# Token mixing in groups of 512 columns, convolution sums in PSUM, and 256-column products throughout a decoder layer

## The chip, the cores and the metric

One Trainium2 chip, of which the kernel uses one core. The metric is the device time of one execution in microseconds. Engines are named as in the profile: PE multiplies matrices, ACT (ScalarE), DVE (VectorE) and POOL (GpSimd) work element by element, SP issues transfers.

## The reference

One decoder layer on 256 tokens of width 2048, in fp32:

```python
f = swiglu_ffn(rms_norm(h, ffn1_pre_g), ffn1_w_gu, ffn1_w_down)        # d_ff 5632
h = h + 0.5 * rms_norm(f, ffn1_post_g)
z = rms_norm(h, mix_pre_g) @ w_in                                      # 2048 x 5120
a, g, q, k, v = split(z, 5 x 1024)
conv_out = silu(layer_norm(causal_depthwise_conv31(a * sigmoid(g))))   # 1024 channels
attn = moba_attention(rope(q), rope(k), v)       # 8 heads; 256 tokens are one block: causal attention
h = h + rms_norm(concat(conv_out, attn) @ w_out, mix_post_g)
h = h + rms_norm(memory_cross_attention(rms_norm(h), rms_norm(mem)), xattn_post_g)
f = swiglu_ffn(rms_norm(h, ffn2_pre_g), ffn2_w_gu, ffn2_w_down)
return h + 0.5 * rms_norm(f, ffn2_post_g)
```

## The kernel before

All weights come from HBM once, as tiles of 128 x 1024 fp32 (`raw`, 512 KB each), through one queue of SP. Each tile is split into two parts in a reduced format that PE multiplies in one pass: `hi` is written by ACT (`split_hi`, L177 without and L179 with a gain per row), `lo` = raw - `hi` by DVE (`split_lo`, L193 without, L195 with a gain). Activations are split likewise (chunks `ck`, parts 0 and 1). A product of the layer is then three on PE: hi with hi, hi with lo, lo with hi. `Weights` prepares `hi` three tiles and `lo` two tiles ahead of use.

A **step** is one weight tile: `step(mm, k)` takes it, issues its 24 products of 256 columns (or the like) and then lets a background queue (`Background`, `bg`) issue pieces for the other engines: pieces of the main queue up to the next `cut`, and then taps of the convolution as far as a credit per engine allows. Each engine executes its instructions in the order in which they are issued.

The stages are gate-up of the first feed-forward network (22 groups of 512 columns, weights stationary, `gate_up`), its down projection (tokens stationary, `proj` and `down`, two halves of 44 tiles), a boundary with residual, norm and transposes (`boundary`, with key products of the cross-attention as fillers), token mixing, cross-attention, and the second feed-forward network.

In gate-up the first two groups use `proj_T`, products of 256 columns. All others multiply a `hi` weight with both activation parts at once, 512 columns (L636), and `lo` with part 0, 256 columns (L638). The halves are added afterwards (`add_parts`, L596 and L597).

Token mixing multiplies four groups for the gated product (`glu_group`, 256 channels each), then queries and keys of four heads (1024 columns, four PSUM banks), all values (four banks), and queries and keys of the other four heads. The convolution has 31 taps on 8 tiles of 128 channels. For the even tiles a tap is one DVE operation on SBUF (`tap_dve`, L746: cv = yv * w + cv). For the odd ones ACT multiplies (L756) and POOL adds (L757), through a ring of three products. `queue_ln` normalises the result, `queue_rope` rotates queries and keys, `queue_heads` runs the attention of four heads in stages. All of these share the main queue. The output projection (`down`) takes the convolution's 8 tiles first and then the heads.

Of the kernel before, what the change touches and what calls it, by code (L numbers as in the profile page):

```python
# [14 lines left out]
P = 128  # L15
# [12 lines left out]
RAW, HI, LO, TMP = 4, 4, 3, 2  # L28
STEP_DVE, STEP_ACT, STEP_POOL = 1.2, 1.3, 2.4
TAIL = 3  # L30
X_AT = [0, 1, 3, 5]
MEM_AT = [20, 22, 24, 26]
# [10 lines left out]
class Background:  # L43


    def __init__(self):
        self.main = deque()
        self.dve = deque()
        self.pool = deque()
        self.credit = [0.0, 0.0, 0.0]  # L50

    def add(self, fn, dve=0.0, act=0.0, pool=0.0):
        self.main.append((fn, dve, act, pool))

    def cut(self):
        self.main.append(None)

    def urgent(self, pieces):

        for fn, dve, act in reversed(pieces):  # L60
            self.main.appendleft(None)
            self.main.appendleft((fn, dve, act, 0.0))
# [5 lines left out]
    def step(self):  # L68
        self.credit = [min(c + d, d) for c, d in zip(self.credit, (STEP_DVE, STEP_ACT, STEP_POOL))]
        while self.main:  # L70
            p = self.main.popleft()
            if p is None:
                break
            p[0]()
            self.spend(*p[1:])
        while self.dve and self.credit[0] > 0:
            self.dve.popleft()()
            self.spend(0.4, 0.0, 0.0)
        while self.pool and self.credit[1] > 0 and self.credit[2] > 0:
            self.pool.popleft()()  # L80
            self.spend(0.0, 0.4, 0.7)

    def flush(self):
        while self.main:
            p = self.main.popleft()
            if p is not None:
                p[0]()
# [136 lines left out]
def layer_kernel(ctx: ExitStack, tc: tile.TileContext, x, mem, eye, consts, smalls, post_g, xt, memt,  # L224
# [15 lines left out]
    def chunk(dt=F32R):  # L240
        if dt == F32R:
            return ap.tile([P, 4, 2, 256], F32R, tag="chunk", bufs=15, name="ck")
        return ap.tile([P, 2048], F32, tag="chunk", bufs=15, name="cf")
# [51 lines left out]
    for n in range(32):  # L295
        u = 2 * (n % 8)
        W.add(w_in[n // 16, n % 16], [S_GM + u, S_GM + u + 1])
    for g in (3, 2, 4):
        for k in range(KT):
            W.add(w_in[g, k], [S_GM + k])  # L300
    for hf in range(2):
        for k in range(KT):
            W.add(w_out[hf, k])
            kv_extra(1, hf, k, KV_AT2)
# [47 lines left out]
    class Rows:  # L352


        def __init__(self, src, key=None):
            self.src = src
            self.key = key
            self.xT = [None] * 4
# [11 lines left out]
        def hi(self, t, c):  # L370
            make_hi(self.part(t, c, 0), self.ps[t, c])

        def lo(self, t, c):
            make_lo(self.part(t, c, 1), self.ps.pop((t, c)), self.part(t, c, 0))
# [43 lines left out]
    def proj_T(regions, first, last, hi, lo, xk, parts_first=False):  # L418
# [10 lines left out]
    def proj(pss, first, last, hi, lo, xk, t, n0=0):  # L429

        xs = [xk[:, f, t * P:(t + 1) * P] for f in (0, 1, 0)]
        for n, ps in enumerate(pss):
            for o in (0, 256):
                c = slice((n0 + n) * 512 + o, (n0 + n) * 512 + o + 256)
# [822 lines left out]
```

## Time and profile before

| | |
|---|---|
| median of 3 runs | 1967.59 us (1964.88 to 1969.87) |
| profiled execution, its own time | 1969.58 us |
| its span, first to last instruction | 1967.8 us |
| PE, DVE, ACT, POOL busy | 97%, 65%, 56%, 10% of the span |
| mean granted clock of PE | 0.995 |
| gate-up of the first network | 57.5 to 500.2 us |
| its down projection | 500.2 to 740.0 us |
| token mixing with its output projection | 753.3 to 1130.8 us |

Products on PE are pipelined: the time of one overlaps the next, so the pace of a stretch is read from the starts of its instructions or from their number in a stretch, not from the mean time of one. An instruction that crosses the edge of a stretch counts in both.

### The profile page before, as it was taken

Reading aid. Unit: us, or ns where it says so; the run is one execution under the profiler, and the core shown is the slowest. Engines: PE = TensorE matmul, PEld = TensorE weight load, DVE = VectorE, ACT = ScalarE, POOL = GpSimd, SP = SyncE. Lnnn points to the kernel's source line nnn. Section 1 sums busy time; section 2 is a strip of 40 time slices with the busy share of each in tenths; the row PEclk is TensorE's granted clock in tenths of the full one; section 3 lists DMA queues with packets and bytes.
Section 4 is the critical chain, followed back from the end, with each engine's and each line's share of the span. In section 5 each row is a group of like instructions: output and inputs, shape, how many; then the busy total and the mean of one; then the engine's idle time right before and its main releaser. Section 6 shows DMA issues by size and latency. Waiting matters only on the chain.

```text
span 1967.8 us, 34797 instructions
## 1 busy us (share of the span) xinstructions
PE 1913.8 (97%) x13818; PEld 1794.8 (91%) x13818; DVE 1269.5 (65%) x1774; ACT 1098.5 (56%) x1793; POOL 205.0 (10%) x192
## 2 busy tenths in 40 slices
PE   8999999999999999888999999999999999999998
PEld 8888888888999999877899999988888888899998
DVE  5666666666545557999767676666666666654444
ACT  6655555555434646766465565655556555543433
POOL 0000000000000000768401000000000000000000
PEclk9999999999999999999999999999999999999999
DMA  8555566555656774444555653555655555666564
GB/s 286 191 192 187 190 192 193 189 189 191 215 194 194 265 246 139 131 149 140 168 164 163 223 179 122 171 190 189 191 191 192 189 188 191 209 198 194 194 193 149
DMA packets 102116, 369.98 MB, mean 188 GB/s; under 512 B 11456, under 2 KB 11712, under 8 KB 101184
## 3 DMA queue, kind: packets, MB, share of 16 engines
q1 hardware_dynamic: 100944, 361.00, 56.5%
q10 hardware_dynamic: 1008, 6.75, 0.9%
q8 instruction: 108, 1.77, 0.4%
q14 instruction: 56, 0.46, 0.1%
HBM read 365.61 MB, written 2.10 MB: 187 GB/s over the span
## 4 chain that ended last, share of the span: by engine, by line
PE 89%; DVE 5%; issue 2%; POOL 2%; ACT 1%; DMA 1%; SPq 0%; DVEq 0%; POOLq 0%; ACTq 0%
PE ps L436 31%; PE ps L636 30%; PE ps L638 15%; PE ps L423 7%; PE ps L426 3%; DVE lo L195 3%; DVE cv L746 2%; POOL cv L757 1%; PE ps L339 0%; DMA raw<-in_f_gu_dram 0%; ACT hi L179 0%; PE ps L1079 0%; DMA raw<-in_xt_dram 0%; PE ps L1077 0%; PE ps L1078 0%
## 5 line engine op out<-in xcount | busy, mean ns | idle before, releaser
L195 DVE SCALAR_TENSOR_TENSOR lo<-raw,sm,hi 128x512 fp32r<-128x512 f32 (+1 forms) x830 | 636.8, 806 | 336.6 <-issue 249.1
L179 ACT ACTIVATE hi<-raw,sm 128x512 fp32r<-128x512 f32 (+1 forms) x830 | 576.2, 740 | 379.4 <-PE ps L636 223.1
L636 PE MATMUL ps<-ck,hi 128*128 128x512 f32 x2560 | 693.6, 393 | 0.0
L436 PE MATMUL ps<-hi,ck 128*128 128x256 f32 x3584 | 619.0, 279 | 1.3 <-ACT ck L347 1.0
L436 PEld LDWEIGHTS ps<-hi,ck 128*128 128x128 f32 x3584 | 545.7, 189 | 2.0 <-ACT ck L347 1.2
L436 PE MATMUL ps<-lo,ck 128*128 128x256 f32 x1792 | 499.5, 279 | 8.6 <-DVE lo L195 6.8
L636 PEld LDWEIGHTS ps<-ck,hi 128*128 128x128 f32 x2560 | 434.8, 188 | 54.7
L193 DVE TENSOR_TENSOR lo<-raw,hi 128x1024 fp32r<-128x1024 f32 x216 | 265.7, 1231 | 266.4 <-PE ps L436 230.8
L638 PEld LDWEIGHTS ps<-ck,lo 128*128 128x128 f32 x2560 | 388.4, 188 | 53.7
L638 PE MATMUL ps<-ck,lo 128*128 128x256 f32 x2560 | 400.0, 278 | 0.0
L177 ACT ACTIVATE hi<-raw 128x1024 fp32r<-128x1024 f32 x216 | 229.1, 1062 | 289.1 <-PE ps L436 241.0
L436 PEld LDWEIGHTS ps<-lo,ck 128*128 128x128 f32 x1792 | 339.5, 189 | 9.8 <-DVE lo L195 7.6
L423 PE MATMUL ps<-ck,hi 128*128 128x256 f32 x1664 | 230.1, 284 | 9.5 <-ACT hi L140 5.6
L423 PEld LDWEIGHTS ps<-ck,hi 128*128 128x128 f32 x1664 | 210.9, 190 | 10.8 <-ACT hi L140 5.6
L605 POOL TENSOR_TENSOR tmp<-tmp,rb 128x512 f32<-128x512 f32 x44 | 58.5, 1329 | 1127.3 <-ACT tmp L604 1108.0
L426 PE MATMUL ps<-ck,lo 128*128 128x256 f32 x832 | 130.4, 285 | 23.4 <-DVE lo L195 23.4
L426 PEld LDWEIGHTS ps<-ck,lo 128*128 128x128 f32 x832 | 111.5, 190 | 28.3 <-DVE lo L195 28.3
L757 POOL TENSOR_TENSOR cv<-cv,cf 128x255 f32<-128x255 f32 (+14 forms) x120 | 106.3, 887 | 31.9 <-ACT cf L756 23.5
L746 DVE SCALAR_TENSOR_TENSOR cv<-yv,cf,cv 128x255 f32<-128x255 f32 (+14 forms) x120 | 85.0, 708 | 2.7
L597 DVE TENSOR_TENSOR tmp<-ps,tmp 128x256 f32<-128x256 f32 x160 | 60.1, 417 | 10.8 <-ACT tmp L596 10.8
L756 ACT ACTIVATE cf<-yv,cf 128x255 f32<-128x255 f32 (+14 forms) x120 | 54.6, 487 | 16.5 <-POOL cv L757 16.1
L347 ACT ACTIVATE ck<-tmp 128x512 fp32r<-128x512 f32 x44 | 27.8, 632 | 50.2 <-DVE tmp L608 50.2
(136 smaller groups left out, 837.7 us busy)
## 6 DMA issues: line engine op xcount, KB each, us to landing
raw<-in_f_gu_dram SPq DMA_DIRECT2D x351, 512.0 KB, 4.2
raw<-in_f_down_dram SPq DMA_DIRECT2D x176, 512.0 KB, 4.3
raw<-in_w_in_dram SPq DMA_DIRECT2D x80, 512.0 KB, 3.5
raw<-in_w_out_dram SPq DMA_DIRECT2D x32, 512.0 KB, 3.6
cf<-in_post_g_dram ACTq DMA_DIRECT2D x4, 1024.0 KB, 6.6
raw<-in_x_k_dram SPq DMA_DIRECT2D x8, 512.0 KB, 4.4
raw<-in_x_q_dram SPq DMA_DIRECT2D x8, 512.0 KB, 4.1
raw<-in_x_o_dram SPq DMA_DIRECT2D x8, 512.0 KB, 4.2
```

The costliest lines, as they stand in the source:

```text
L177: self.nc.scalar.activation(dst, src, AF.Copy)
L179: self.nc.scalar.activation(dst, src, AF.Copy, scale=g)
L193: self.nc.vector.tensor_tensor(dst, src, hi.bitcast(F32), ALU.subtract)
L195: self.nc.vector.scalar_tensor_tensor(dst, src, g, hi.bitcast(F32), ALU.mult, ALU.subtract)
L423: nc.tensor.matmul(ps[:, o:o + 256], hi[:, j * P:(j + 1) * P], xk[:, f, :], start=first and o == 0 and f == 0, stop=False, skip_group_chec ...
L426: nc.tensor.matmul(ps[:, o:o + 256], lo[:, j * P:(j + 1) * P], xk[:, 0, :], start=False, stop=last, skip_group_check=True)
L436: nc.tensor.matmul(ps[:, o:o + 256], xs[i], w[:, c], start=first and o == 0 and i == 0, stop=last and i == 2, skip_group_check=True)
L597: nc.vector.tensor_tensor(s[:, c], ps[:, 0:256], s[:, c], ALU.add)
L636: nc.tensor.matmul(ps, hi[:, w], xk, start=k == 0, stop=False, skip_group_check=True)
L638: nc.tensor.matmul(ps[:, 256:512], lo[:, w], xk[:, 0, :], start=False, stop=k == KT - 1, skip_group_check=True)
L746: nc.vector.scalar_tensor_tensor(cv[:, ct, s:], yv[:, ct, :S - s], w, cv[:, ct, s:], ALU.mult, ALU.add)
L757: nc.gpsimd.tensor_tensor(cv[:, ct, s:], cv[:, ct, s:], pr[:, :S - s], ALU.add)
```

## The change

- **Gate-up:** all groups use `proj_T`, 256 columns a product, three products per weight tile of 128 x 128 and two PSUM banks a group. `add_parts` is gone: DVE multiplies straight from PSUM.
- **Order in `proj_T`:** for each PSUM region the three products (hi, hi, lo) follow each other. Before, eight `hi` products came first and four `lo` products after them.
- **Halved products:** at given steps (`HALVED`), products number 0, 4 and 8 are split into two of 128 columns each: in gate-up in the groups 1 and 2, in each down projection at two tiles of the first half, in each mixing group at one tile. These are 54 products.
- **Mixing groups:** ten groups of 512 columns with 8 tiles each: four gated ones, then queries and keys of two heads twice, values of four heads, and the same again. The pre-norm gain of mixing goes into the activations (`Rows`, four operations of 128 columns per part in place of one of 512), so that weight tiles are split without a gain.
- **Convolution:** the even channel tiles sum up in two PSUM banks (`tap_acc`): ACT writes tap 1 with the bias, DVE adds the taps 2 to 30 in PSUM and writes the last sum with tap 0 to SBUF.
- **Background:** two lanes (`lanes`), one for the normalisation of the convolution, other rates per step (`MIX_RATE`, `TAP_DVE`), and pieces cut so that each engine's part of a chain has a step of its own. The product `yv` and the last add of the rotation move from POOL to DVE.
- **Output projection:** the heads 0 to 3 come first, then the convolution, then the heads 4 to 7 (`OUT_ORDER`).
- Four temporaries in place of two, 16 chunks in place of 15, and a smaller scratch space for transfers make room.

```diff
+MIX_RATE = (1.45, 1.6, 2.5)
+TAP_DVE = 0.47
+OUT_ORDER = [8, 9, 10, 11, 0, 1, 2, 3, 4, 5, 6, 7, 12, 13, 14, 15]
+HALVED = (0, 4, 8)
...
-    for n in range(32):
-        u = 2 * (n % 8)
-        W.add(w_in[n // 16, n % 16], [S_GM + u, S_GM + u + 1])
-    for g in (3, 2, 4):
-        for k in range(KT):
-            W.add(w_in[g, k], [S_GM + k])
+    for n in range(10):
+        for u in range(8):
+            W.add(w_in[n, u])
...
+            for k in range(4):
+                nc.scalar.activation(hi[:, k], src[:, k], AF.Copy, scale=self.gain_of(c, k))
...
-        order = [(f, r) for f in range(2) for r in enumerate(regions)]
-        if not parts_first:
-            order = [(f, r) for r in enumerate(regions) for f in range(2)]
-        for f, (j, (ps, o)) in order:
-            nc.tensor.matmul(ps[:, o:o + 256], hi[:, j * P:(j + 1) * P], xk[:, f, :],
-                             start=first and o == 0 and f == 0, stop=False, skip_group_check=True)
-        for j, (ps, o) in enumerate(regions):
-            nc.tensor.matmul(ps[:, o:o + 256], lo[:, j * P:(j + 1) * P], xk[:, 0, :],
-                             start=False, stop=last, skip_group_check=True)
+        order = [(r, i) for r in enumerate(regions) for i in range(3)]
+        if parts_first:
+            order = [(r, i) for i in range(3) for r in enumerate(regions)]
+        for n, ((j, (ps, o)), i) in enumerate(order):
+            w = 128 if n in halved else 256
+            for a in range(0, 256, w):
+                nc.tensor.matmul(ps[:, o + a:o + a + w], (hi, hi, lo)[i][:, j * P:(j + 1) * P], xk[:, i % 2, a:a + w],
+                                 start=first and o == 0 and i == 0 and a == 0, stop=last and i == 2,
+                                 skip_group_check=True)
...
+                    at = HALVED if t == 0 and (hf, n) in ((0, 1), (0, 5)) else ()
+                    proj(pss[t], n == 0, n == nk - 1, hi, lo, lhs(order[n]), t, 0, at)
...
-                    for ps, w in zip(pss, ws):
-                        nc.tensor.matmul(ps, hi[:, w], xk, start=k == 0, stop=False, skip_group_check=True)
-                    for ps, w in zip(pss, ws):
-                        nc.tensor.matmul(ps[:, 256:512], lo[:, w], xk[:, 0, :], start=False, stop=k == KT - 1,
-                                         skip_group_check=True)
+                    proj_T(regions_of(pss), k == 0, k == KT - 1, hi[:, e * 512:], lo[:, e * 512:], rows.x(k),
+                           g == k == 0, HALVED if e == 0 and (g, u) in ((1, 1), (2, 1)) else ())
...
+    def tap_acc(ct, s):
+
         w = whalf[:, ct * TAPS + TAPS - 1 - s:ct * TAPS + TAPS - s]
-        if s == 0:
-            nc.vector.tensor_scalar(cv[:, ct, :], yv[:, ct, :], w,
-                                    sm[:, S_CB + ct:S_CB + ct + 1], ALU.mult, ALU.add)
+        a = acc[ct // 4][:, (ct % 4) * 128:(ct % 4) * 128 + 256]
+        b = sm[:, S_CB + ct:S_CB + ct + 1]
+        if s == 1:
+            nc.scalar.activation(a[:, 1:], yv[:, ct, :S - 1], AF.Identity, scale=w, bias=b)
+            nc.scalar.activation(a[:, 0:1], b, AF.Copy)
         else:
-            nc.vector.scalar_tensor_tensor(cv[:, ct, s:], yv[:, ct, :S - s], w, cv[:, ct, s:],
-                                           ALU.mult, ALU.add)
+            o = a[:, s:] if s else cv[:, ct, :]
+            nc.vector.scalar_tensor_tensor(o, yv[:, ct, :S - s], w, a[:, s:], ALU.mult, ALU.add)
...
+    for c in range(2):
+        for p in range(2):
+            pss = in_group(lambda u: norm_conv(c == 1 and p == 1 and u == 5))
+            if p == 0:
+                qk.append(chunk(F32))
+            queue_rope(pss, p, qk[c])
+        v_group(c, lambda u: norm_conv(False))
+        queue_heads(range(4 * c, 4 * c + 4))
     post = Post(1, 1.0)
```

DVE in the mixing stage, in the second gated group, before: two low halves of a weight tile with a gain (`lo`), then three taps into the SBUF sums (`cv`), and so on.

```order
L195 SCALAR_TENSOR_TENSOR lo<-raw,sm,hi 128x512 x2
L746 SCALAR_TENSOR_TENSOR cv<-yv,cf,cv 128x245
L746 SCALAR_TENSOR_TENSOR cv<-yv,cf,cv 128x244
L746 SCALAR_TENSOR_TENSOR cv<-yv,cf,cv 128x243
L195 SCALAR_TENSOR_TENSOR lo<-raw,sm,hi 128x512 x2
```

The same place now, around the gate (L789) and the product (L793, L794) of the second group.

```order
L197 TENSOR_TENSOR lo<-raw,hi 128x1024
L756 SCALAR_TENSOR_TENSOR ps<-yv,cf,ps 128x241
L756 SCALAR_TENSOR_TENSOR ps<-yv,cf,ps 128x240
L756 SCALAR_TENSOR_TENSOR ps<-yv,cf,ps 128x239
L197 TENSOR_TENSOR lo<-raw,hi 128x1024
L789 TENSOR_TENSOR tmp<-ps,rb 128x512
L756 SCALAR_TENSOR_TENSOR ps<-yv,cf,ps 128x238
L756 SCALAR_TENSOR_TENSOR ps<-yv,cf,ps 128x237
L197 TENSOR_TENSOR lo<-raw,hi 128x1024
L793 SCALAR_TENSOR_TENSOR tmp<-tmp,ps 128x512
L794 TENSOR_TENSOR yv<-tmp,rb 128x512
L197 TENSOR_TENSOR lo<-raw,hi 128x1024
```

One operation of 1024 columns stands where two of 512 stood; there are still three taps a step, on `ps` now; a step with a gate or a product has fewer or none.

PE in gate-up, before, at the step from the second group (L423, L426) to the third (L636, L638).

```order
L423 MATMUL ps<-ck,hi 128x256 x8
L426 MATMUL ps<-ck,lo 128x256 x4
L636 MATMUL ps<-ck,hi 128x512 x4
L638 MATMUL ps<-ck,lo 128x256 x4
L636 MATMUL ps<-ck,hi 128x512 x4
```

PE now, in the second group, at a step with halved products (128x128).

```order
L443 MATMUL ps<-ck,lo 128x256
L443 MATMUL ps<-ck,hi 128x128 x2
L443 MATMUL ps<-ck,hi 128x256
L443 MATMUL ps<-ck,lo 128x256
L443 MATMUL ps<-ck,hi 128x256
L443 MATMUL ps<-ck,hi 128x128 x2
L443 MATMUL ps<-ck,lo 128x256
L443 MATMUL ps<-ck,hi 128x256 x2
L443 MATMUL ps<-ck,lo 128x128 x2
L443 MATMUL ps<-ck,hi 128x256 x2
L443 MATMUL ps<-ck,lo 128x256
```

Each `lo` product now follows its two `hi` products, and three of these twelve are two instructions each.

DVE at the end of mixing, now: the last centred and scaled piece of the convolution (L949), its low parts (L351), and the values of the second half (L1022) that the heads 4 to 7 need.

```order
L949 TENSOR_TENSOR cv<-cv,cf 128x512
L351 TENSOR_TENSOR ck<-cv,ck 128x2x256
L197 TENSOR_TENSOR lo<-raw,hi 128x1024
L351 TENSOR_TENSOR ck<-cv,ck 128x2x256
L197 TENSOR_TENSOR lo<-raw,hi 128x1024
L351 TENSOR_TENSOR ck<-cv,ck 128x2x256
L197 TENSOR_TENSOR lo<-raw,hi 128x1024
L1022 TENSOR_SCALAR cf<-ps,scal_9256 128x512
L1022 TENSOR_SCALAR cf<-ps,scal_9262 128x512
```

The last low part stands behind the 82nd low half of mixing, whose input projection has 80 tiles; the low halves run two tiles ahead of PE.

## Rows read from the trace of the kernel before

**Rows 1.** The page, part 1: busy time, share of the span, instructions.

```profile
PE 1913.8 (97%) x13818; PEld 1794.8 (91%) x13818; DVE 1269.5 (65%) x1774; ACT 1098.5 (56%) x1793; POOL 205.0 (10%) x192
```

**Rows 2.** Stretches: length, busy time (instructions) of each engine, clock, DMA share, GB/s.

```profile
100.00:150.00 50.00, 50.00 (x292) 43.90 (x291) 33.42 (x55) 29.02 (x52) 2.62 (x2) 1.00 0.59 192
550.00:600.00 50.00, 50.00 (x443) 50.00 (x443) 22.70 (x19) 19.44 (x19) 0.00 (x0) 1.00 0.60 195
...
800.00:850.00 50.00, 41.75 (x336) 39.92 (x336) 49.26 (x66) 32.05 (x64) 33.43 (x39) 1.00 0.45 142
850.00:900.00 50.00, 39.98 (x320) 38.12 (x320) 49.22 (x57) 35.86 (x63) 40.23 (x44) 1.00 0.43 144
900.00:950.00 50.00, 38.77 (x275) 36.95 (x276) 46.26 (x48) 29.67 (x46) 40.63 (x38) 0.90 0.38 127
950.00:1000.00 50.00, 50.00 (x410) 49.75 (x410) 39.09 (x44) 26.66 (x30) 8.87 (x4) 0.97 0.60 190
```

**Rows 3.** Waits, 790 to 925 us: total us, times, longest.

```profile
PE ps L426 <- DVE lo L195: 23.4, 24, 1.4
```

**Rows 4.** Groups by shape, DVE, 790 to 925 us: count, busy us, mean ns.

```profile
L195 DVE SCALAR_TENSOR_TENSOR lo<-raw,sm,hi 128x512 fp32r<-128x512 f32 x38 | 38.2, 1044 | 0.0
...
L783 DVE TENSOR_TENSOR tmp<-ps,rb 128x512 f32<-128x512 f32 x3 | 2.1, 684 | 0.0
L787 DVE SCALAR_TENSOR_TENSOR tmp<-tmp,ps 128x512 f32<-128x512 f32 x3 | 2.0, 679 | 0.0
```

**Rows 5.** Groups, DVE: gate-up 100 to 480, down 510 to 650, all taps.

```profile
L195 DVE SCALAR_TENSOR_TENSOR lo<-raw,sm,hi 128x512 fp32r<-128x512 f32 x276 | 195.0, 748 | 126.8 <-issue 107.0 <-ACT ck L347 14.1 <-PE ps L638 5.7
L597 DVE TENSOR_TENSOR tmp<-ps,tmp 128x256 f32<-128x256 f32 x70 | 26.3, 417 | 4.4 <-ACT tmp L596 4.4
...
L193 DVE TENSOR_TENSOR lo<-raw,hi 128x1024 fp32r<-128x1024 f32 x51 | 62.5, 1226 | 73.5 <-PE ps L436 72.1 <-issue 0.9 <-ACT tmp L344 0.6
...
L746 DVE SCALAR_TENSOR_TENSOR cv<-yv,cf,cv 128x255 f32<-128x255 f32 (+14 forms) x120 | 85.0, 708 | 2.7
```

**Rows 6.** Timeline of DVE, 939 to 952 us: start, us, instruction.

```profile
939.30 3.61 DVE L746 SCALAR_TENSOR_TENSOR cv<-yv,cf,cv 128x243 f32<-128x243 f32 x3
...
949.58 1.45 DVE L746 SCALAR_TENSOR_TENSOR cv<-yv,cf,cv 128x237 f32<-128x237 f32 x3
```

**Rows 7.** Timeline of PE: early gate-up, start and end of its 512-column part, later stretch.

```profile
33.03 1.11 PE L423 MATMUL ps<-ck,hi 128*128 128x256 f32 x8
33.97 0.63 PE L426 MATMUL ps<-ck,lo 128*128 128x256 f32 x4
34.44 1.11 PE L423 MATMUL ps<-ck,hi 128*128 128x256 f32 x8
...
57.49 1.08 PE L636 MATMUL ps<-ck,hi 128*128 128x512 f32 x4
...
500.17 0.41 PE L436 MATMUL ps<-hi,ck 128*128 128x256 f32 x2
...
1247.12 1.07 PE L423 MATMUL ps<-ck,hi 128*128 128x256 f32 x8
1248.03 0.62 PE L426 MATMUL ps<-ck,lo 128*128 128x256 f32 x4
1248.48 1.07 PE L423 MATMUL ps<-ck,hi 128*128 128x256 f32 x8
```

**Rows 8.** Stretches of 10 us: down projection, value projection.

```profile
510.00:520.00 10.00, 10.00 (x90) 10.00 (x90) 4.63 (x5) 3.88 (x4) 0.00 (x0) 1.00 0.58 181
969.00:979.00 10.00, 10.00 (x88) 10.00 (x86) 7.86 (x9) 5.66 (x7) 6.01 (x3) 1.00 0.54 175
```

**Rows 9.** Timeline of PE: transposes of 128 columns at the boundary.

```profile
742.94 1.04 PE L339 MATMUL ps<-ident,h 128*128 128x128 f32 x8
743.73 0.72 PE L423 MATMUL ps<-ck 128*128 128x256 f32 x4
```

**Rows 10.** Groups by shape, ACT, whole span: high parts from PSUM.

```profile
L347 ACT ACTIVATE ck<-ps 128x512 fp32r<-128x512 f32 x24 | 13.8, 588 | 21.6 <-PE ps L339 21.6
...
L347 ACT ACTIVATE ck<-ps 128x256 fp32r<-128x256 f32 x12 | 4.3, 375 | 4.6 <-PE ps L866 4.2 <-PE ps L1099 0.5
```

More of the change, by code (lines that the diff above doesn't have):

```diff
@@ L718, in layer_kernel @@
     last = down(KF, lambda k: hT[k // 4][:, k % 4], post, ffn1_hook)
-    rows = Rows(h_rows)
+    rows = Rows(h_rows, gain=S_GM)
     boundary(post, last, rows, kv_k(0))
+    bg.rate = MIX_RATE
     mx = chunk(F32)
@@ L787, in product, with taps @@
             nc.vector.scalar_tensor_tensor(box[0], box[0], 1.0, pss[0], ALU.add, ALU.mult)
[L788 removed]
+            nc.vector.tensor_tensor(yv[:, 2 * q:2 * q + 2, :], two(box[0]), bc2(rows.rb), ALU.mult)
+        def taps():
+            gated.append(q)
+            for s in [*range(2, TAPS), 0]:
+                bg.dve.append(lambda s=s: tap_acc(2 * q, s))
             for s in range(TAPS):
[L790 removed]
@@ L931, in act, with first, split @@
                                      bias=sm[:, S_LB + ct:S_LB + ct + 1])
-        bg.add(sums, pool=3.7)
-        bg.cut()
+        def first():
+            cT[0:2] = [chunk(), chunk()]
+        def split(i, low):
+            c = slice(2 * (i % 2), 2 * (i % 2) + 2)
+            if not low:
+                make_hi(cT[i // 2][:, c, 0, :], cv[:, 2 * i:2 * i + 2, :])
+                return
+            make_lo(cT[i // 2][:, c, 1, :], cv[:, 2 * i:2 * i + 2, :], cT[i // 2][:, c, 0, :])
+        bg.lane = 1
+        bg.add(sums, dve=0.6, pool=1.2)
         bg.cut()
@@ L971, in layer_kernel @@
+        bg.cut()
+        bg.add(first)
+        for i in range(6):
+            if i < 4:
+                bg.add(lambda i=i: act(i), dve=0.7, act=1.0)
+            if 0 < i < 5:
+                bg.add(lambda i=i: split(i - 1, False), act=0.6)
+            if i > 1:
+                bg.add(lambda i=i: split(i - 2, True), dve=0.7)
+            bg.cut()
+        bg.lane = 0
     for q in range(4):
         glu_group(q)
-    pss = in_group()
-    qk.append(chunk(F32))
-    queue_rope(pss, qk[0], False)
@@ L977, in layer_kernel, with norm_conv @@
-    vps = [[bank() for _ in range(2)] for _ in range(2)]
-    def mm_v(k, hi, lo):
-        for t in range(2):
-            proj(vps[t], k == 0, k == KT - 1, hi, lo, rows.x(k), t)
-    normed = False
-    for k in range(KT):
-        step(mm_v, k)
-        if not normed and (k == 10 or not (bg.dve or bg.pool)):
+    normed = []
+    def norm_conv(last):
+        if len(gated) == 4 and not normed and (last or not (bg.dve or bg.pool)):
             bg.flush_taps()
             queue_ln()
-            normed = True
@@ L1007, in layer_kernel, with v_group, mm, v_rows @@
-    post = Post(1, 1.0)
-    last = down(KT, lambda k: cT[k // 4][:, k % 4], post)
+            normed.append(True)
+    def v_group(c, hook):
+        vps = [bank() for _ in range(2)]
+        def mm(u, hi, lo):
+            for e in range(2):
+                k = 2 * u + e
+                for t in range(2):
+                    proj([vps[t]], k == 0, k == KT - 1, hi[:, e * 512:], lo[:, e * 512:], rows.x(k), t)
+        for u in range(8):
+            step(mm, u)
+            hook(u)
+        if c == 0:
+            vms.append(chunk(F32).rearrange("p (t c) -> p t c", t=2))
+        def v_rows(t):
+            nc.vector.tensor_scalar(vms[0][:, t, c * 512:(c + 1) * 512], vps[t], rows.rs[t], None, ALU.mult)
+        for t in range(2):
+            bg.add(lambda t=t: v_rows(t), dve=0.6)
+        bg.cut()
@@ L1011, in layer_kernel @@
+    last = down(KT, lambda k: cT[k // 4][:, k % 4], post, done_hook, order=OUT_ORDER)
+    bg.rate = (STEP_DVE, STEP_ACT, STEP_POOL)
     rows = Rows(h_rows)
```

277 lines of the change are left out of this document (134 added, 143 removed).

## The prediction

> **What bounds the kernel now.** I read the page's engine totals first: the reader is to see PE busy 97% of the span, so only PE's pace and PE's pauses can be worth much [rows 1]. Then the stretches of 50 us. A gate-up stretch and a down stretch leave PE no pause; four stretches of the mixing stage do, and DVE is busy 49.3 of 50 us in two of them [rows 2]. The waits there name the releaser: PE's products with the low half of a weight tile wait for DVE's L195, 23.4 us in 24 waits [rows 3]. So two things are to be priced: the pace of products in gate-up, and DVE's load in the mixing stage.
>
> Pace. Products of 256 columns run at two rates. Twelve take 1.41 us in the first groups of gate-up (33.03 to 34.44) and 1.36 us in a later stretch of the same line (1247.12 to 1248.48) [rows 7]: 117.5 ns and 113.3 ns each. A down stretch starts 90 in 10 us; the value projection, the same code, 88 [rows 8]. The rate stays through a stretch and changes at its edges. The granted clock is 1.00 on both sides [rows 8], the 2.4 GHz level, so it isn't the clock.
>
> Loss in mixing. A step is one weight tile, 24 products. From 800 to 1000 us, 336 + 320 + 275 + 410 = 1341 products started; at 117.5 ns they need 157.6 us, so 42.4 of 200 us are lost. In 900 to 950 the granted clock averages 0.90 after PE's pauses: part of it at 1.2 GHz, whose price is inside the 42.4 [rows 2].
>
> **The change, part by part.**
>
> Gate-up, all products 256 columns. From 57.49 to 500.17 us the first gate-up does 1280 pairs (512 + 256 columns): 345.8 ns a pair, 1.383 us for four [rows 7]. A pair becomes three products of 256: 340.0 ns at the fast rate, 352.5 at the slow one. That is -5.8 or +6.7 ns times 1280, twice (the second feed-forward network repeats it): **-14.9 or +17.2 us**. The row shows twelve fast products (3072 columns) in 1.36 us where four pairs, the same columns in eight products, take longer: a third product carries no price of its own there. The Trainium skill (TensorE: Matmul & The Clock Gate, Back-to-back issue gap) gives a warm product N/2.4 + 2.5 ns: 215.8 + 109.2 for a pair, 327.5 for three, so by it the edit costs 2.5 ns 2560 times, 6.4 us, instead of gaining. The rows are slower than that formula either way, and the sum goes by the rows. I take the fast rate: the new order (high, high, low in one PSUM region, then the next) is the down projection's, where it held. Against it: the weights stay the stationary operand, as in the slow stretch of rows 7. What the two gates drop on ACT and DVE (copies and adds of halves) lies beside PE, which never paused there.
>
> Halved products: 54 are split into two of 128 columns (12 in gate-up, 18 in the three down projections, 24 in mixing). Nearest row: eight transposes of 128 columns take 0.79 us, 0.10 us each [rows 9], so a pair costs 0.20 for 0.113: +0.09 x 54 = **+4.9 us**. The low bound is 0 (half the columns, half the time), the high one 10, twice the row's excess. They are the only disturbance put inside otherwise even stretches, so the rate after them may differ from that before.
>
> Mixing, DVE per step. Before: two low halves of 512 columns at 1.044 us and three taps at 0.708 us: 4.21 us, against 2.82 us of products [rows 4, 5]. Both prices are swollen: the low half takes 0.748 in gate-up [rows 5], and three taps take 3.61 us at 939 but 1.45 at 949, ten us later [rows 6]. But in the stretch where low halves are swollen, DVE's operations with one operand in PSUM take 684 and 679 ns for 512 columns [rows 4], less than the swollen 1.044. So what swells is the pair of SBUF operands. The new taps read the sum from PSUM and write it back; no row has DVE writing PSUM. The nearest is DVE's add of a PSUM and an SBUF operand, 256 columns: 0.417 us [rows 5]; the far bound is today's 0.708. The low half, now without a gain, is one operation of 1024 columns: 1.226 us in the down stretch [rows 5], swollen by 1.044/0.748 at most 1.71. Per step: 2.48 us at best, 1.71 + 3 x 0.417 = 2.96 likely at worst, 1.71 + 3 x 0.708 = 3.83 if PSUM doesn't help; PE needs 2.72 at the fast rate. 124 taps at three a step make 41 steps: 0, 10 or 45 us left of the 42.4. I take 6, the middle of the first two and 1 for PSUM banks (two are held by the sums; PE may wait for one while heads overlap a group). **-36.4 us**. If PE's DVE wait goes, the next that can be late is ACT, whose products for the Pool taps wait for Pool ahead of the next weight's high half in the queue.
>
> Order around it: the normalisation runs in a lane of its own, and in the changed order its last piece on DVE stands at about the first tile of the output projection, which needs the convolution only at its fifth; the heads 4 to 7, needed at the thirteenth, end just before it. So I add no wait. The gated product and the rotation's last add move from Pool to DVE (4 + 8 operations of about 0.68 us, about 8 us) and take the place of taps in their steps, over more steps.
>
> Mixing, rate: in eight groups the steps after the halved products (6 x 24 x 8 = 1152) can run 4.2 ns faster: 4.8 us; the heads' own products cut two of these groups up, so **-3.5**.
>
> Rows with gains: a high part of 512 columns becomes four of 128. From 0.588 and 0.375 us for 512 and 256 columns [rows 10] one of 128 is about 0.27, four 1.08: +0.49 us on ACT, and about as much on DVE, four times in a row at the boundary ahead of mixing, where key products lie beside it; later ones are hidden behind steps in which the shorter weight pieces give back as much. I take **+1** (bounds 0 and 4).
>
> Transfers carry the same tiles of 512 KB; nothing there.
>
> Sum: -14.9 - 36.4 - 3.5 + 4.9 + 1 = -48.9 us, on 1969.58 us, the profiled execution's own time (span 1967.8): 1920.7. That execution lies 2.0 above the median of the runs, 1967.59, so against it **1918.7 us**.
>
> **Rivals.**
> 1. The slow rate stays in gate-up and mixing: +17.2 instead of -14.9, and the 3.5 gone: 1954.3. For it: the line of rows 7 runs slow where weights are stationary. Against: the same line has run fast.
> 2. In between: one gate-up fast, one slow (16 us later), 1935. A small price for each added product would look alike. By the 2.5 ns of the Trainium skill (same page and section) the time would be 1940.
> 3. DVE stays the bound: PSUM taps cost what SBUF taps did, 3.83 us a step, and the 36.4 are not got: 1955. Against: 684 and 679 ns in the swollen stretch.
> 4. **Slower.** The halved products leave PE at the slow rate wherever they stand, the down and output projections included, which are fast now: 4992 products x 4.2 ns = 21.0 us more, on top of rival 1: 1975. It decides only when both down projections are slow as well as gate-up (8.9 us each); with one the time stays under that of before. For it: both rates occur in that code [rows 8].
>
> **How the numbers follow.** Chances: forecast 0.56, rival 1 0.18, rival 2 0.13, rival 3 0.07, rival 4 0.06. About 0.3% (5.9 us) is what a measurement of this kernel can tell from no change. The forecast's own range is 1905 (no loss left in mixing, halved products and boundary free, the fast rate through the heads too) to 1931 (10 left, both other bounds high). The range reaches up to rivals 2 and 1: 1905 to 1957; what is outside is rival 4, half of rival 3 and the edges, 0.2. Faster: the forecast, rivals 1 and 2 nearly whole, half of 3: 0.88; same 0.06; slower 0.06.
>
> **What would show it.** Gate-up in a stretch of 50 us: some 443 products at the fast rate, 428 at the slow. DVE's PSUM taps: about 0.42 us and alike whether Pool works or not; near 0.7, rival 3. PE's waits for DVE in mixing: under 8 us. Down stretches: still 443; 428 says rival 4. Halved products: 0.20 us a pair. Wrong would be the forecast above all through the rate, which no row explains, and through a wait of PE for PSUM banks in the heads.

## The result and the profile after

The changed kernel takes **1912.38 us** (median; 1910.12 to 1913.52), the kernel before in the same comparison 1967.17 us: a ratio of 0.972 (95% interval 0.9703 to 0.9736), 54.8 us less. The forecast was 1918.7 us. The profiled execution of the changed kernel took 1911.87 us, its span is 1909.9 us. Of the executions told of below one, of the kernel with the old order, ran at a mean granted clock of 0.75 and took 2366.63 us; its ratio leaves that one out.

The page's engine totals after, which answer to [rows 1]:

```profile
PE 1887.3 (99%) x16436; PEld 1881.2 (98%) x16436; DVE 1181.8 (62%) x1611; ACT 1046.3 (55%) x1625; POOL 203.4 (11%) x182
```

PE has 2618 instructions more than before and is busy 26.5 us less. The stretches, with the columns of [rows 2]:

```profile
100.00:150.00 50.00, 50.00 (x444) 50.00 (x443) 30.30 (x44) 27.11 (x42) 3.76 (x3) 1.00 0.59 193
550.00:600.00 50.00, 50.00 (x444) 50.00 (x443) 22.65 (x19) 19.88 (x19) 0.00 (x0) 1.00 0.60 195
800.00:850.00 50.00, 50.00 (x444) 50.00 (x443) 47.65 (x67) 39.00 (x70) 45.16 (x44) 1.00 0.55 180
850.00:900.00 50.00, 48.77 (x419) 48.08 (x419) 47.04 (x65) 39.98 (x67) 44.83 (x42) 1.00 0.54 179
900.00:950.00 50.00, 49.68 (x415) 48.95 (x415) 41.82 (x70) 32.51 (x68) 26.41 (x28) 1.00 0.53 176
950.00:1000.00 50.00, 49.62 (x419) 49.05 (x418) 41.82 (x53) 35.70 (x53) 11.90 (x7) 1.00 0.57 194
1000.00:1050.00 50.00, 50.00 (x432) 49.73 (x431) 27.86 (x38) 25.03 (x46) 0.00 (x0) 1.00 0.50 169
```

Gate-up runs at 444 products in 50 us, the fast rate, and mixing issues 1697 products from 800 to 1000 us where it issued 1341 [rows 2]. The granted clock is 1.00 throughout, also from 900 to 950 us, where it was 0.90. PE's waits from 790 to 925 us, which were 23.4 us in 24 waits [rows 3], are 1.5 us in three:

```profile
PE ps L443 <- DVE lo L197: 1.2, 2, 1.1
PE ps L457 <- DVE lo L197: 0.3, 1, 0.3
```

DVE's groups in the same stretch, all shapes of a line together for the taps (answers to [rows 4, 5]):

```profile
L197 DVE TENSOR_TENSOR lo<-raw,hi 128x1024 fp32r<-128x1024 f32 x47 | 68.8, 1464 | 1.3 <-ACT hi L181 1.3
L756 DVE SCALAR_TENSOR_TENSOR ps<-yv,cf,ps 128x245 f32<-128x245 f32 (+28 forms) x105 | 49.2, 468 | 2.5 <-ACT ps L753 0.2
```

A tap takes 468 ns where it took 708; a low half of 1024 columns takes 1464 ns where two of 512 took 2088. Over the whole stage no tap takes longer than 488 ns (shortest, median and longest in ns, after the count):

```profile
L756 DVE SCALAR_TENSOR_TENSOR ps<-yv,cf,ps x116: 446/469/488, 782.9 to 937.2; 128x254 f32<-128x254 f32 x4, 128x253 f32<-128x253 f32 x4, 128x252 f32<-128x252 f32 x4, 128x251 f32<-128x251 f32 x4
```

Where the time went, by stage. The table is worked out from the starts of PE's first and last products of each stage in the traces (us; the first column counts from the span's start). It holds the runs of the next section too:

| kernel | first gate-up, to | down | boundary, mixing, output projection | cross-attention, second gate-up | last down |
|---|---|---|---|---|---|
| before | 500.2 | 239.8 | 390.8 | 588.9 | 239.3 |
| after | 492.2 | 240.9 | 347.4 | 580.4 | 240.4 |
| no product halved | 508.3 | 240.0 | 346.8 | 598.7 | 248.4 |
| one halved per place | 491.6 | 240.2 | 346.3 | 598.5 | 239.8 |
| down projections whole | 491.9 | 249.3 | 347.8 | 579.2 | 248.6 |
| old order, halved | 491.0 | 240.9 | 346.9 | 581.8 | 240.4 |
| old gate-up | 499.8 | 240.8 | 347.8 | 588.3 | 240.2 |
| taps in SBUF | 491.0 | 240.7 | 370.8 | 581.3 | 240.4 |
| gain on the weights | 491.2 | 242.1 | 360.2 | 579.9 | 240.4 |
| both of these | 492.6 | 240.7 | 379.8 | 579.9 | 240.4 |
| output in old order | 491.3 | 240.9 | 347.9 | 580.7 | 240.2 |
| more places | 492.4 | 240.5 | 347.1 | 581.7 | 240.1 |
| before, new gate-up | 491.4 | 249.1 | 390.8 | 579.8 | 248.6 |
| before, gate-up and downs | 490.9 | 240.9 | 391.5 | 579.9 | 240.4 |

So -16.5 us in the two stretches with gate-up, +2.2 in the two down projections and -43.4 in mixing: -57.7, between two profiled executions of which before's lies 2.4 us above its median and after's 0.5 below. The terms of the prediction made -48.9.

### The profile page after: what moved, and what is told of

It is laid out like the page before. It is cut to its first block, busy times and chain, and to the rows that moved or that the text cites. A ratio compares the mean times of both kernels' runs of the same rounds, so it can differ in the third digit from the quotient of the medians.

```text
span 1909.9 us, 39740 instructions
## 1 busy us (share of the span) xinstructions
PE 1887.3 (99%) x16436; PEld 1881.2 (98%) x16436; DVE 1181.8 (62%) x1611; ACT 1046.3 (55%) x1625; POOL 203.4 (11%) x182
## 4 chain that ended last, share of the span: by engine, by line
PE 88%; DVE 5%; ACT 2%; issue 2%; POOL 1%; DMA 1%; SPq 0%; DVEq 0%; POOLq 0%; ACTq 0%
PE ps L443 54%; PE ps L457 32%; DVE lo L197 2%; POOL cv L766 1%; DVE ps L756 1%; DMA raw<-in_f_gu_dram 1%; DMA raw<-in_x_v_dram 1%; ACT hi L181 1%; PE ps L340 0%; DVE h L501 0%; DVE cf L827 0%; ACT hi L183 0%; DVE lo L199 0%; PE ps L857 0%; PE ps L1141 0%
## 5 line engine op out<-in xcount | busy, mean ns | idle before, releaser
L443 PE MATMUL ps<-ck,hi 128*128 128x256 f32 x6808 | 1168.3, 277 | 8.0 <-ACT hi L144 6.7
L443 PEld LDWEIGHTS ps<-ck,hi 128*128 128x128 f32 x6808 | 1027.5, 188 | 9.3 <-ACT hi L144 6.7
L443 PE MATMUL ps<-ck,lo 128*128 128x256 f32 x3404 | 939.2, 277 | 2.1 <-DVE lo L197 1.2
L199 DVE SCALAR_TENSOR_TENSOR lo<-raw,sm,hi 128x512 fp32r<-128x512 f32 x718 | 517.7, 763 | 356.3 <-issue 334.4
L183 ACT ACTIVATE hi<-raw,sm 128x512 fp32r<-128x512 f32 x718 | 479.4, 716 | 374.0 <-PE ps L443 223.4
L443 PEld LDWEIGHTS ps<-ck,lo 128*128 128x128 f32 x3404 | 638.3, 188 | 3.4 <-DVE lo L197 1.8
L197 DVE TENSOR_TENSOR lo<-raw,hi 128x1024 fp32r<-128x1024 f32 x296 | 374.8, 1267 | 294.2 <-PE ps L457 231.4
L457 PE MATMUL ps<-lo,ck 128*128 128x256 f32 (+1 forms) x1798 | 496.3, 277 | 0.3 <-DVE lo L197 0.3
L181 ACT ACTIVATE hi<-raw 128x1024 fp32r<-128x1024 f32 x296 | 312.8, 1059 | 322.4 <-PE ps L457 245.9
L765 ACT ACTIVATE cf<-yv,cf 128x255 f32<-128x255 f32 (+14 forms) x120 | 56.1, 490 | 22.7 <-POOL cv L766 22.4
L756 DVE SCALAR_TENSOR_TENSOR ps<-yv,cf,ps 128x254 f32<-128x254 f32 (+28 forms) x116 | 54.4, 469 | 2.7 <-ACT ps L753 0.2
L351 DVE TENSOR_TENSOR ck<-tmp,ck 128x512 fp32r<-128x512 f32 x44 | 30.1, 684 | 0.0
```

What stands on the lines that cost most here:

```text
L181: self.nc.scalar.activation(dst, src, AF.Copy)
L183: self.nc.scalar.activation(dst, src, AF.Copy, scale=g)
L197: self.nc.vector.tensor_tensor(dst, src, hi.bitcast(F32), ALU.subtract)
L199: self.nc.vector.scalar_tensor_tensor(dst, src, g, hi.bitcast(F32), ALU.mult, ALU.subtract)
L351: nc.vector.tensor_tensor(lo, src, hi.bitcast(F32), ALU.subtract)
L443: nc.tensor.matmul(ps[:, o + a:o + a + w], (hi, hi, lo)[i][:, j * P:(j + 1) * P], xk[:, i % 2, a:a + w], start=first and o == 0 and i == 0 ...
```

## Experiments on PE's rate

Theory: the halved products put PE on the fast rate. Rival: the order of the products does. A second question is whether the gain of gate-up stands by itself.

**No product halved.**

```diff
-HALVED = (0, 4, 8)
+HALVED = ()
```

> The changed kernel with no product halved, everything else as changed. Theory T1 (the halved products put PE on the fast rate): without them the gate-ups run at the slow rate, some 428 products instead of 444 in 50 us, which is 7680 products x 4.2 ns = 32 us, less 6.5 us for the 54 pairs that are gone: about 1938 us; up to 1955 if the down projections and the mixing groups are slow too. Rival T1' (the order high, high, low in one region is enough): gate-up stays at 444 and the time falls by the price of the pairs, to about 1906 us.

Measured: 1951.32 us (1940.77 to 1953.95); ratio to before 0.990 (0.9874 to 0.9926). Stretches of its first gate-up, first down and last down:

```profile
100.00:150.00 50.00, 50.00 (x426) 50.00 (x426) 28.90 (x43) 25.62 (x39) 2.58 (x2) 1.00 0.53 184
510.00:560.00 50.00, 50.00 (x444) 50.00 (x443) 23.64 (x21) 20.29 (x20) 1.29 (x1) 1.00 0.57 203
1700.00:1750.00 50.00, 50.00 (x427) 50.00 (x426) 23.03 (x20) 19.39 (x19) 0.00 (x0) 1.00 0.54 186
```

Both gate-ups are slow, and the last down with them, all at clock 1.00: the table has 16.1, 18.3 and 8.0 us more than after. The order alone doesn't give the fast rate. The first down is fast without any halved product, at 444. Mixing is slow too and takes no longer, 346.8 us against 347.4. One of the four executions took 1940.77 us, some 10 us less than the others; it has no trace, so which of its stages was fast isn't known.

**One halved product per place.**

```diff
-HALVED = (0, 4, 8)
+HALVED = (8,)
```

> The changed kernel with one halved product at each place instead of three (18 in all, the one of number 8, a low product). If one is enough to set the rate, and a pair costs 0.12 us more than a whole product, as the trace after the change shows (0.34 to 0.38 us for three): 36 x 0.12 = 4.2 us less, about 1908 us, with 444 products in 50 us of gate-up. If the number, or where it stands in the step, matters: slow gate-ups, about 1940 us.

Measured: two runs at 1908.83 and 1909.76 us, four from 1925.71 to 1927.94, so the median of 1926.36 lies in the larger of two groups. In the profiled execution (first gate-up, mixing, second gate-up):

```profile
100.00:150.00 50.00, 50.00 (x444) 50.00 (x443) 30.86 (x44) 27.67 (x43) 3.92 (x3) 1.00 0.56 197
800.00:850.00 50.00, 50.00 (x428) 50.00 (x427) 47.61 (x68) 39.66 (x72) 45.08 (x45) 1.00 0.51 179
1300.00:1350.00 50.00, 50.00 (x427) 50.00 (x426) 29.67 (x44) 26.61 (x41) 2.60 (x2) 1.00 0.54 189
```

The second gate-up stayed slow, 18.1 us longer than after, which is the distance of the two groups; that it was fast in the two short executions is likely but not shown, as neither has a trace. One halved product can set the rate, but doesn't do it each time. The two short executions are about 3 us faster than after, near the expected 4.2.

**The old order, with the halved products.**

```diff
-        order = [(r, i) for r in enumerate(regions) for i in range(3)]
+        order = [(r, i) for r in enumerate(regions) for i in range(2)] + [(r, 2) for r in enumerate(regions)]
```

> The changed kernel with the old order in the weight-stationary products (high, high for each region, then the four low products), the products number 0, 4 and 8 halved as changed. Theory T1 (the halved products set the rate whatever the order): 444 products in 50 us of gate-up, about 1912 us. Rival T1' (the order matters too): gate-up at 428, +32 us, about 1944 us, or fast in only one of the two networks, 1928 us.

Measured: 1911.52 us, the changed kernel's time; ratio to before 0.9706 (0.9686 to 0.9725). Its first gate-up:

```profile
100.00:150.00 50.00, 50.00 (x444) 50.00 (x443) 30.70 (x46) 27.10 (x42) 3.90 (x3) 1.00 0.58 196
```

With the first run this settles it for gate-up: beside halved products the order is worth nothing, and without them the new order doesn't give the fast rate. (A whole gate-up of 256-column products in the old order without halved ones was not run.)

**The kernel before with the new gate-up alone** (gate-up, its gates, the product order and the halved products of gate-up as changed; the `proj` of the down projections as before).

```diff
+HALVED = (0, 4, 8)
...
+                    proj_T(regions_of(pss), k == 0, k == KT - 1, hi[:, e * 512:], lo[:, e * 512:], rows.x(k),
+                           g == k == 0, HALVED if e == 0 and (g, u) in ((1, 1), (2, 1)) else ())
...
```

> The kernel before with the new gate-up alone: all its products 256 columns in the order high, high, low, the gates straight from PSUM, and the halved products of gate-up; mixing, down projections and everything else as before. If the gate-up's term stands by itself: 12 pairs at 0.12 us on -14.9 us, so about 13.5 us less than before, 1954 us, with 444 products in 50 us. If the rate needs something else of the change: +17 us, 1985 us, with 428.

Measured: 1969.64 us; ratio 1.0004 (0.9994 to 1.0013). Neither of the two: the gate-ups did gain, and the down projections gave it back. First gate-up, first down, last down:

```profile
100.00:150.00 50.00, 50.00 (x443) 50.00 (x442) 31.11 (x45) 27.75 (x43) 3.89 (x3) 1.00 0.57 197
520.00:570.00 50.00, 50.00 (x427) 50.00 (x426) 21.94 (x18) 18.85 (x18) 0.00 (x0) 1.00 0.55 187
1740.00:1790.00 50.00, 50.00 (x427) 50.00 (x426) 21.69 (x18) 18.61 (x18) 0.00 (x0) 1.00 0.55 186
```

By the table, -8.8 and -9.1 us in the stretches with gate-up, +9.3 and +9.3 us in the down projections, whose code is that of before: there they ran at 443 [rows 2], here at 427.

**The same with halved products in the down projections.**

```diff
...
+                    at = HALVED if t == 0 and (hf, k) in ((0, 1), (0, 5)) else ()
+                    proj(pss[t], k == 0, k == nk - 1, hi, lo, lhs(k), t, 0, at)
```

> The kernel before with the new gate-up and, beside what the run with gate-up alone had, the halved products of the three down projections. That run gained nothing: its gate-ups ran at 443 products in 50 us and both down projections at 427, which were at 443 before. If the whole-256 gate-up leaves the down projections at the slow rate and their own halved products bring them back: two times some 8.5 us less, plus 18 x 0.12 = 2.1 us, so about 1955 us, and 443 products in both. If something else of the change made the down projections fast: 1969 us or a little more, with 427.

Measured: 1953.35 us (1952.23 to 1954.88); ratio 0.9912 (0.9888 to 0.9936). Both down projections are at the fast rate again:

```profile
520.00:570.00 50.00, 50.00 (x444) 50.00 (x443) 22.49 (x19) 19.23 (x19) 0.00 (x0) 1.00 0.57 192
1740.00:1790.00 50.00, 50.00 (x444) 50.00 (x443) 22.95 (x19) 19.69 (x19) 0.00 (x0) 1.00 0.57 196
```

**The changed kernel with whole products in the down projections.**

```diff
-                    at = HALVED if t == 0 and (hf, n) in ((0, 1), (0, 5)) else ()
+                    at = ()
```

> The changed kernel with no halved product in the three down projections (18 fewer); gate-up and mixing as changed. Their trace shows each down projection slow at its start and fast after the first place. If they come to the fast rate by themselves, as the first did with no product halved at all: 18 x 0.12 = 2 us less, 1910 us. If a place of its own is needed, 2112 x 4.2 ns = 8.9 us for each slow network's and 3.2 us for the output projection's, up to 21 us in all: 1919 to 1931 us, with 428 products in 50 us.

Measured: 1928.24 us (1927.31 to 1930.38), the upper case: 8.4 and 8.2 us more in the two feed-forward networks' down projections, 427 products in 50 us, here in the first:

```profile
550.00:600.00 50.00, 50.00 (x427) 50.00 (x426) 21.30 (x18) 18.73 (x18) 0.00 (x0) 1.00 0.56 186
```

The output projection costs the same with and without (347.8 against 347.4 for its stage).

**The changed kernel with the old gate-up** (`gate_up`, `queue_gate` and `add_parts` of before; the halved products stay in the second group).

```diff
...
+                    for ps, w in zip(pss, ws):
+                        nc.tensor.matmul(ps, hi[:, w], xk, start=k == 0, stop=False, skip_group_check=True)
+                    for ps, w in zip(pss, ws):
+                        nc.tensor.matmul(ps[:, 256:512], lo[:, w], xk[:, 0, :], start=False, stop=k == KT - 1,
+                                         skip_group_check=True)
...
```

> The changed kernel with the gate-up of before (pairs of 512 and 256 columns from the third group on, halves added by ACT and DVE); the halved products stay in the second group, the down projections and mixing. If the terms add up: the prediction's 14.9 us back, less 0.7 us for six pairs, so about 1926 us. If gate-up's gain is worth more in this surrounding (the queue of ACT and DVE behind it): 1930 us or more; if less, under 1920 us.

Measured: 1928.04 us (1926.17 to 1929.08), 15.7 above after. The terms add up.

**More places.**

```diff
-                    at = HALVED if t == 0 and (hf, n) in ((0, 1), (0, 5)) else ()
+                    at = HALVED if t == 0 and (hf, n) == (0, 1) else ()
...
-                           g == k == 0, HALVED if e == 0 and (g, u) in ((1, 1), (2, 1)) else ())
+                           g == k == 0, HALVED if e == 0 and (g, u) in ((0, 1), (1, 1), (2, 1)) else ())
...
+                   HALVED if u == 1 and e == 0 else ())
...
+                 HALVED if hf == 0 and k == 1 else ())
```

> The changed kernel with three halved products also where its trace still shows the slow rate: in the first group of each gate-up, in the queries of the cross-attention and in its output projection; and without the second place of each down projection, where PE was fast already and three pairs cost 0.35 us. By the trace after the change: 3 x 0.35 us saved, and 4.2 ns for each of some 220, 190 and 190 products made fast, 2.5 us, less 1.4 us for the four places: about 2 us less than the changed kernel, 1910 us. Rival (the second place of a down projection holds the rate): the last down projection slow, 1919 us or more.

Measured: 1912.39 us, no change against 1912.38: a miss, though a small one. Without their second place the down projections take 0.4 and 0.3 us less and stay fast, which refutes its rival. But in the first network's first group and in the cross-attention's output projection the rate stayed slow behind the new pairs: products start 118 and 120 ns apart there, as after (76 and 86 in 10 us; PE also pauses 0.9 us in the first of these). No version here beats the changed kernel by more than the measurement can tell.

## Experiments on mixing

Theory: both reliefs of DVE are needed, the taps in PSUM and the low halves without a gain. Rival: one alone is enough.

**Taps back in SBUF.**

```diff
-    acc = [bank() for _ in range(2)]
...
-        a = acc[ct // 4][:, (ct % 4) * 128:(ct % 4) * 128 + 256]
+        a = cv[:, ct, :]
```

> The changed kernel with the sums of the even channel tiles back in SBUF; all else as changed. Theory T2 (both reliefs of DVE are needed): with three taps at 0.708 us (their mean before) and a low half of 1.44 us a step takes DVE 3.56 us against 2.72 us of products: 116 taps, 39 steps, +33 us, about 1945 us, and PE waits for the low halves again. Rival (the low half in one operation is enough): at most 10 us more, under 1922 us.

Measured: 1936.02 us (1934.64 to 1937.52), 23.6 above after. DVE's groups and the stretches from 800 to 900 us:

```profile
L755 DVE SCALAR_TENSOR_TENSOR cv<-yv,cf,cv 128x238 f32<-128x238 f32 (+14 forms) x70 | 49.1, 703 | 1.5
L197 DVE TENSOR_TENSOR lo<-raw,hi 128x1024 fp32r<-128x1024 f32 x29 | 45.2, 1557 | 0.0
```

```profile
800.00:850.00 50.00, 43.63 (x358) 42.00 (x357) 49.08 (x57) 35.74 (x64) 38.95 (x41) 1.00 0.46 156
850.00:900.00 50.00, 43.56 (x352) 41.35 (x350) 49.29 (x56) 32.75 (x58) 36.40 (x36) 1.00 0.42 150
```

DVE is full again and PE short of work. The taps run from 781 to 960 us, beside 54 low halves; after the change from 783 to 938, beside 54 as well: 24 us more, all of the difference. The expectation of 33 was too high because it put three taps into each step. 120 taps to 54 tiles are 2.2, the steps with a gate or a rotation having fewer.

**The gain back on the weights.**

```diff
-            W.add(w_in[n, u])
+            W.add(w_in[n, u], [S_GM + 2 * u, S_GM + 2 * u + 1])
...
-    rows = Rows(h_rows, gain=S_GM)
+    rows = Rows(h_rows)
```

> The changed kernel with the norm's gain of the mixing stage on its weight tiles again (two low halves of 512 columns in place of one operation of 1024, two high halves likewise) and none on the activations; the taps stay in PSUM. Theory T2 (both reliefs are needed): two at 1.04 us and three taps at 0.47 us make 3.5 us a step against 2.72: +25 to +32 us, about 1940 us. Rival (taps in PSUM are enough, because the gain's operation is swollen by the SBUF taps alone and takes 0.75 us without them): 2.9 us a step, +5 to +8 us, under 1921 us.

Measured: 1923.45 us (1922.04 to 1924.32), 11.1 above after, between the two cases. In the same stretch:

```profile
L199 DVE SCALAR_TENSOR_TENSOR lo<-raw,sm,hi 128x512 fp32r<-128x512 f32 x63 | 60.0, 993 | 0.0
L756 DVE SCALAR_TENSOR_TENSOR ps<-yv,cf,ps 128x236 f32<-128x236 f32 (+28 forms) x74 | 34.6, 468 | 1.6
```

Without the SBUF taps a low half with a gain still takes 993 ns, nowhere near gate-up's 748 [rows 5]: it isn't the taps that swell it. The trace shows beside what it swells: the 69 such halves from 735 to 1080 us during which Pool has no operation take 645 to 754 ns, the 91 beside one 737 to 1792.

**Both undone.**

> The changed kernel with both reliefs of DVE in mixing undone: the even tiles' sums in SBUF and the gain on the weight tiles. Alone they cost 24 and 11 us. If DVE is simply the bound and each operation adds its time: 35 us and, since the first 6 to 8 us of DVE's excess are no longer hidden, some more: two low halves at 1.04 us and three taps at 0.71 make 4.2 us a step against 2.72, 39 steps, 58 us: 1947 to 1970 us. If the two share one cause (a low half with gain is only swollen beside SBUF taps, and each fills what the other leaves): 1936 us, as with the taps alone.

The edit is that of the last two runs together. Measured: 1943.97 us (1942.80 to 1944.17), 31.6 above after; 24 and 11 make 35, so the two nearly add, and both reliefs are needed. Two later stretches of it, for what comes below:

```profile
900.00:950.00 50.00, 42.46 (x338) 39.96 (x337) 49.36 (x68) 31.56 (x61) 27.77 (x32) 1.00 0.44 148
1000.00:1050.00 50.00, 50.00 (x419) 49.63 (x419) 39.11 (x63) 32.16 (x61) 1.75 (x1) 1.00 0.60 209
```

**The output projection in the order of before.**

```diff
-OUT_ORDER = [8, 9, 10, 11, 0, 1, 2, 3, 4, 5, 6, 7, 12, 13, 14, 15]
+OUT_ORDER = list(range(16))
```

> The changed kernel with the output projection in the order of before (the convolution's eight tiles, then the heads). In the trace after the change the last low part of the convolution ends at 985.75 us and the output projection begins at 986: if the order is worth nothing, 1912 us, within 2. If the first tiles then wait for the normalisation's end, or the heads 0 to 3 and 4 to 7 behind it run into PE: 3 to 6 us more.

Measured: 1912.10 us (1909.96 to 1912.56): worth nothing, the first of the two cases. PE waits for no other engine from 980 to 1080 us: the first tiles find the normalisation done.

## Why the prediction came out as it did

**Gate-up** was forecast at -14.9 us, less about 1.1 for its 12 halved products. Measured: -16.5 in the two stretches that hold it, and 15.7 when it is undone. The size was right, the reason for it wrong, so that the size came out is luck. The step that took the fast rate because the new order is that of the down projection, where it held, fell: with halved products the order makes no difference, and without them gate-up is slow in the new order. The prediction did name the halved products as the only disturbance in even stretches, without drawing the conclusion that they set the rate.

**The down projections** were to stay at 443, and do, at 443 to 444, but only through their own places. The prediction held them to be fast already and the halved products there to be pure cost. In fact a gate-up of 256-column products that runs at the fast rate leaves them at the slow one, 9.3 us each, as much as gate-up gains: so it was at the start of all 21 down projections behind such a gate-up, by the starts in the traces of all the runs here. Behind the three such gate-ups that ran slow, two down projections began fast, the first one of the kernel with no product halved among them. The slow down projections of rival 4 thus come from the other side: they are what happens without the halved products, not because of them.

**Halved products** were priced at 0.09 us a pair, 4.9 us. From the starts in the trace after, twelve products with three pairs take 0.34 to 0.38 us longer than at the fast rate: 0.12 a pair, 6.3 us for 54 (mixing has them in eight of its ten groups). The nearest row, transposes of 128 columns, was close. The two halves start 58 ns apart, the next product 113 ns later, the one behind it another 169 ns later: 340 ns for what is two products, 227 ns, elsewhere.

**Mixing** is where the total was missed. The terms made -36.4 for DVE, -3.5 for the rate, +1 for the rows with gains and +2.7 for its and the output projection's halved products, -36.2 together; measured -43.4. Three things are in this:
- DVE's price per operation was right: taps 468 ns (417 taken, and 446 to 488 over the whole stage, beside Pool or not), low halves 1464 (1226 to 1710 given). Undoing both reliefs costs 31.6 us, 32.4 by the table's stage, a little under the 36.4.
- The rate and the halved products together are worth nothing there. With no product halved, or one, mixing ran near 427 products in 50 us and its stage took 346.8 and 346.3 us, no more than after. By the starts in the traces, after has 1164 more products of this stage at the fast rate than the kernel with no product halved, about 5.0 us; its 30 pairs there cost 3.6 us, and PE, which without them waits for no low half (850 to 900 us: 50.00 busy, 426 products), waits 1.5 us. The prediction's -3.5 and +2.7 for this were near.
- 11.0 us are not the two reliefs (43.4 less 32.4), and the output projection's order is none of them. About half of them is the clock. Before, PE had three waits of 1.9 to 2.2 us, and behind each of them products of 256 columns started 213 ns apart, the lower level of the clock (1.2 of 2.4 GHz), where the same code runs at 113 ns elsewhere:

```profile
923.22 0.58 PE L436 MATMUL ps<-lo,ck 128*128 128x256 f32 x1 [1.93 <-DVE lo L195]
939.43 0.46 PE L436 MATMUL ps<-lo,ck 128*128 128x256 f32 x1 [2.18 <-DVE lo L195]
949.71 0.49 PE L436 MATMUL ps<-lo,ck 128*128 128x256 f32 x1 [2.12 <-DVE lo L195]
```

```profile
923.00:930.00 7.00, 6.78 (x34) 6.78 (x35) 6.86 (x10) 4.62 (x6) 3.08 (x3) 0.55 0.48 152
930.00:937.00 7.00, 7.00 (x64) 7.00 (x63) 3.93 (x6) 2.40 (x5) 6.06 (x4) 1.00 0.47 150
```

From 923 to 954 us 57 products ran so: an estimated 5.7 us. With both reliefs undone the clock stays at 1.00, though PE pauses there too (900 to 950 us: 42.46 busy). The prediction had this price inside its 42.4, so its 36.4 stand against 32.4 and 5.7. For the rest there is a sign: the prediction counted the loss from 800 to 1000 us only, but before PE also stood still from 1000 to 1050:

```profile
1000.00:1050.00 50.00, 46.84 (x381) 45.59 (x380) 35.08 (x54) 30.28 (x57) 5.97 (x4) 1.00 0.47 150
```

That row is of the kernel before: 3.2 us without work for PE, and 381 products where both undone, whose stage begins 7 us earlier, has 419 and no pause. So these 11 us come from the rest of the change to mixing: groups of 512 columns, the second lane, the rates per step, the moves from Pool to DVE. Which of them kept the clock up, and which removed the pause, was not tried and stays open.

What is late next was named: ACT's products for the Pool taps wait for Pool, 22.4 us (the page's group of them, after):

```profile
L765 ACT ACTIVATE cf<-yv,cf 128x255 f32<-128x255 f32 (+14 forms) x120 | 56.1, 490 | 22.7 <-POOL cv L766 22.4
```

Another piece of ACT's comes late for DVE: in DVE's timeline after (start, us, instruction) it stands still from 866 us before the rotation's product, until ACT's copies for it are done. PE's longest wait of the stage, 1.1 us, follows at 873 us, for a low half that itself took 2.33 us.

```profile
865.03 1.24 DVE L197 TENSOR_TENSOR lo<-raw,hi 128x1024 fp32r<-128x1024 f32 x1
867.90 0.69 DVE L821 TENSOR_TENSOR cf<-ps,cf 128x512 f32<-128x512 f32 x1 [1.63 <-ACT tmp L818]
868.51 0.46 DVE L756 SCALAR_TENSOR_TENSOR ps<-yv,cf,ps 128x237 f32<-128x237 f32 x1
868.88 1.35 DVE L197 TENSOR_TENSOR lo<-raw,hi 128x1024 fp32r<-128x1024 f32 x1
...
872.06 2.33 DVE L197 TENSOR_TENSOR lo<-raw,hi 128x1024 fp32r<-128x1024 f32 x1
```

Rival 3 (PSUM taps no cheaper) is out by the taps' 468 ns. The Trainium skill (SBUF — State Buffer, SBUF: two separate sides) says that DVE's operations with two SBUF inputs contend with a GpSimd operation that reads SBUF, for a port pair that one of the two holds for its whole instruction. The traces agree: the tap with one operand in PSUM does not vary, 446 to 488 ns. A low half has two SBUF operands: after, from 735 to 1076 us, the 62 without an operation of Pool beside them take 1155 to 1228 ns, as in the down projection [rows 5], and the 54 with one 1209 to 2326. The taps in SBUF likewise: before, 450 to 483 ns for 35 without Pool, 455 to 1515 for 85 beside it.

## What to carry to other kernels

Where PE is the bound, count products per stretch before and after in every stage, not only in the one that was edited: a stage can give back in the next what it gained. An edit that speeds PE up in a stage where another engine is nearly full uncovers waits for that engine: take them, and the edit's own price, off the gain. Look for the lower clock behind PE's waits, and price it apart from the waits. When an engine's load is to be cut per step, count how many operations a step holds on average, from the trace, not the most it can hold.

## What was unexpected in the hardware

PE's pace for these products is a state that outlasts its cause: 113.3 ns or about 117.5 for 256 columns, at granted clock 1.00 in both. In the trace after, three products split in two left PE at the fast rate in all 18 steps that have them, whatever the rate ahead of it. In the traces of the other runs they left it slow in 13 of 151 such steps, ten of them in the mixing stage with one or both reliefs of DVE undone. The changed kernel around its first halved step (36.6 us), in 10 us ahead and behind:

```profile
26.00:36.00 10.00, 10.00 (x87) 10.00 (x86) 5.68 (x10) 5.33 (x9) 0.00 (x0) 1.00 0.92 307
38.00:48.00 10.00, 10.00 (x90) 10.00 (x90) 4.80 (x7) 9.12 (x23) 0.00 (x0) 1.00 0.70 241
```

Of the 51 pairs of that trace whose surroundings can be read, 34 are in code where the weights are stationary. None of these turned the rate from fast to slow (21 from fast stayed fast; of 13 from slow six turned fast, at the second or third pair of a step). Where the tokens are stationary, a few products behind a pair start 117 to 122 ns apart, and then the fast rate is back. There a single pair was enough: in the run with one halved product per place, two such places turned slow to fast and four stayed fast. Where the weights are stationary a single pair turned slow to fast in three places of eleven, and its one place ahead of which PE was fast stayed fast. Why the rate has two values, what a pair does to it, and why a fast gate-up of 256-column products is followed by a slow start of the down projection while the pairs of 512 and 256 columns are followed by a fast one in three cases of four, no run here shows. The Trainium skill (TensorE: Matmul & The Clock Gate, Back-to-back issue gap) gives a formula for an isolated warm product, by which 256 columns would take an estimated 109.2 ns, and says that in a stream the weight loads set the spacing too; the traces show neither that time nor a single value, and the measurements decide.
